# Placing an attention's transposes and value products later, and a few steps around them, in a one-core hybrid decoder layer

## The chip, the core and the metric

The kernel runs on one core of one Trainium2 chip. TensorE (PE) multiplies, VectorE (DVE), ScalarE (ACT) and GpSimd (POOL) do the elementwise work, and SyncE (SP) issues every transfer. The metric is the device time of one execution in microseconds, the median over several runs.

## The reference, cut to what matters

One layer of width 2048 over 512 tokens, all in float32. A normalized input is multiplied by one wide matrix, whose columns feed three kinds of branches (twelve heads of a delta-rule recurrence, twelve heads of an attention with a stick-breaking weight, and four pooling groups). The gated branch outputs go through one more matrix and are added to the input.

```
h = rms(x, norm_g)
proj = h @ w_in                      # 2048 columns in, 54 tiles of 128 columns out
pa, pb, pc = split(proj)
ya = rwkv7(token_shift(pa)) * silu(ga)          # per head: state recurrence over 512 steps
yb = pool(pu) * silu(pg)
# attention, per head:
q, k = rms(q, qn_g) * 64**-0.5, rms(k, kn_g)
z = q @ k.T                                      # strictly causal
after = reverse_cumsum(log_sigmoid(-z)) - log_sigmoid(-z)
w = exp(log_sigmoid(z) + after)
yc = (w @ v) * silu(gc)
x = x + concat(ya, yb, yc) @ w_out
```

## The kernel before

**The dense work.** The projection goes tile by tile: 128 columns of `w_in` against all 512 tokens. To reach float32 accuracy each operand is split into a high and a low part, and `three` (L454) issues three products for one: high by high, high by low, low by high. In the trace they are `pj<-hh,wh`, `pj<-hl,wh` and `pj<-hh,wl`. The first three tiles use weights that are split at the start. Each of the other 54 tiles takes two blocks of weights (128 x 1024 elements), so there are 108 blocks, each of 8 x 3 = 24 matmuls of 128 x 512; 32 blocks of `w_out` follow with the same count (`oacc`). Blocks are counted here from 0, the first one behind the three first tiles.

**A block's weights.** `split_weights` (L445) issues the load `raw` on SP's queue (two buffers), the cast `wh` on ACT (three buffers) and the remainder `wl = raw - wh` on DVE (two buffers). `weights(i)` (L477) asks for block i and block i+1, at a high scheduling priority (`AHEAD`). A buffer of `raw` is free again when the `wl` made from it is done, and a buffer of `wl` is free when the last matmul of its block has read it.

**The side work.** Everything else is written as Python generators: `begin`, six `rwkv(p)`, six `attention(p)`, four `pooling(g)`. After each dense matmul `pump` (L417) resumes those whose due time has come, and so their matmuls stand between dense matmuls in PE's order. The due time comes from a model of the engines (`Pace`): `need(tiles, tag, margin)` is the time at which the model has the named tiles ready and a bank of PSUM free, and then `margin` microseconds more (`MARGIN` is 2.5). A generator that yields `None` waits for a condition, for instance that the pair before has set a key in `done`. Four groups of banks are used: `pj` 2, `g` 3, `c` 2, `y` 1. The order on the other engines is a scheduler's, by the same program and its priorities; the engines then run their queues in that order.

**The steps around the change.**

- `emit_rstd` (L358) makes the reciprocal root of the row means: four scaled identities `dg` on DVE, a float32 product `rb` on PE, a copy `rstd` on DVE.
- `rwkv(p)`, L562 to L582: squares `sq` of the key, split into `sh` (ACT) and `sl` (DVE), and their sums over a head `ss` on PE. Further down are the products `gm`, DMAs of blocks out of `lt` to a scratch array `s1` and back as `nblk` and `xblk`, and a chain of 60 dependent small operations on DVE in which `pr` and `xblk` take turns (L681 to L687). They invert triangular blocks.
- `attention(p)`, L815 to L924: norm of query and key (`qs`, its split, `qm` on PE), then per head three groups of scores `z`, from each of which come `w`, `n`, `m` (ACT, POOL, two scans on DVE) and at the end the weights `w`. Behind the scores of both heads, in three groups of key blocks, the weights are transposed (`wT` on PE), copied to `wt` (ACT) and multiplied with the values (`o` on PE). The pair's end sets `done[("att", p)]`.

Of the kernel before, what the change touches and what calls it, by code (L numbers as in the profile page):

```python
# [8 lines left out]
F32 = mybir.dt.float32  # L9
# [4 lines left out]
P = 128  # L14
# [39 lines left out]
MARGIN = 2.5  # L54
TIGHT = 2.0
AHEAD = 300
# [161 lines left out]
def hybrid_trunk_kernel(ctx: ExitStack, tc: tile.TileContext, x, xT, w_in, w_out, vecs, consts, up_w, pool_w, out):  # L218
# [5 lines left out]
    def dma(out, in_, queue=nc.sync):  # L224
        pace.transfer(out, in_)
        queue.dma_start(out=out, in_=in_)
# [13 lines left out]
    def name(s):  # L240
        uid[0] += 1
        return f"{s}_{uid[0]}"
# [17 lines left out]
    def gb(s="g"):  # L260
        return bank("g", s)
# [96 lines left out]
    def emit_rstd():  # L358
        rt = cp.tile([P, 3, 4], F32, name="rt")
        ms, y0, t = rt[:, 0, :], rt[:, 1, :], rt[:, 2, :]  # L360
        dve.tensor_tensor(ms, xsum[:, 0, :], xsum[:, 1, :], ALU.add)
        dve.tensor_scalar(ms, ms, 1.0 / D, RMS_EPS, ALU.mult, ALU.add)
        act.activation(y0, ms, AF.Ln)
        act.activation(y0, y0, AF.Exp, scale=-0.5)
        dve.tensor_tensor(t, y0, y0, ALU.mult)
        dve.tensor_tensor(t, ms, t, ALU.mult)
        dve.tensor_scalar(t, t, -0.5, 1.5, ALU.mult, ALU.add)
        dve.tensor_tensor(y0, y0, t, ALU.mult)
        dg = tmp("dg")
        for i in range(4):  # L370
            dve.tensor_scalar(dg[:, i * P:(i + 1) * P], ident, y0[:, i:i + 1], None, ALU.mult)
        rb = gb("rb")
        pe.matmul(rb, ones_c, dg, start=True, stop=True)
        dve.tensor_copy(out=rstd, in_=rb)


# [65 lines left out]

    HK = KT // 2

    def split_weights(src):  # L445
        raw = wp.tile([P, HK * P], F32, tag="raw", bufs=2, name=name("raw"))
        dma(out=raw, in_=src)
        wh = wp.tile([P, HK * P], F32R, tag="wh", bufs=3, name=name("wh"))
        wl = wp.tile([P, HK * P], F32R, tag="wl", name=name("wl"))
        act.copy(out=wh, in_=raw)  # L450
        dve.tensor_tensor(wl, raw, wh.bitcast(F32), ALU.subtract)
        return wh, wl
# [19 lines left out]
    def fetch(i):  # L472
        if i < len(stream) and i not in fetched:
            with tc.high_priority(offset=AHEAD if i > 1 else 60):
                fetched[i] = split_weights(stream[i])

    def weights(i):  # L477
        fetch(i)
        fetch(i + 1)
        return fetched.pop(i)  # L480

    def project(n):
# [71 lines left out]
    def rwkv(p):  # L554
# [18 lines left out]
        mm(av, uph[:, P:2 * P], ad2, True, False)  # L573
        mm(av, upl[:, P:2 * P], ad2, False, True)
        a = sigmoid(av, bias=nvec[:, 6 + p:7 + p])
        yield need(*sqp, tag="g")
        ss = gb("ss")
        block_sum(ss, bone_r, sqp)
        rn = sq
# [233 lines left out]


    def attention(p):  # L815
        while p > 0 and not done.get(("att", p - 1)):
            yield None
        qk = []
        for kind, gain, slot in (("cq", nvec[:, 12:13], "aq"), ("ck", vec[:, V_KN:V_KN + 1], "ak")):
# [4 lines left out]
            sq = tmp("qs")  # L824
            act.activation(sq, raw, AF.Square)
            sqp = split(sq)
            yield need(*sqp, tag="g")
            ms = gb("qm")
            block_sum(ms, bmean_r, sqp)
            y0, t = newton_rsqrt(ms, RMS_EPS, eps_rms, sq)  # L830
# [6 lines left out]
        act.copy(out=kr, in_=k)  # L837
        klo = tmpr("klo")
        dve.tensor_tensor(klo, k, kr.bitcast(F32), ALU.subtract)
        head = []  # L840
        for h in range(2):
            s = slice(h * HD, (h + 1) * HD)
# [42 lines left out]
            if h == 0:  # L885
# [6 lines left out]
                for j in range(4):  # L892
                    transpose(vps[:, j * P:(j + 1) * P], vs[:, j * P:(j + 1) * P])
                act.copy(out=vt, in_=vps.rearrange("p (j c) -> p j c", j=4))

        o = None
        for js, width in (((0,), 512), ((1, 3), 512), ((2,), 256)):
            parts = []
            for h in range(2):
                yield need(*head[h].values(), tag="g", margin=MARGIN + 2.0)  # L900
                tps = gb("wT")
                pos = {}
                off = 0
# [6 lines left out]
                wt = ap.tile([P, T], F32, tag=home, name=name("wt"))[:, 0:width] if home else tmp("wt", width)  # L910
                act.copy(out=wt, in_=tps[:, 0:width])
                parts.append(wt)
            yield need(*parts, vt, tag="g" if o is None else None)
            if o is None:
                o = gb("o")
            for j in js:
# [106 lines left out]

    def begin():
        yield need(xsum, tag="g")
        emit_rstd()
        for n in range(NFIRST):
            finish(n, first[n])

# [134 lines left out]
```

## Time and profile before

| | before |
|---|---|
| median of 3 runs (lowest, highest) | 1008.57 us (1006.39, 1008.71) |
| the profiled execution, its span | 1007.96 us, 1006.1 us |
| PE busy | 978.3 us, 97% of the span |
| weight loads of PE (PEld, beside PE) | 786.9 us |
| DVE busy | 662.2 us, 66% |
| ACT busy | 511.6 us, 51% |
| POOL busy | 140.5 us, 14% |
| granted clock of PE | 0.996 |

The profiled execution is 0.6 us under the median. A matmul's end is modelled: a dense matmul is shown 0.39 us long though the next one starts 0.23 us after it, so the idle time shown in front of a late matmul is shorter than the time by which its start was late. A row of a timeline gives the start, the duration, the engine, the line, the operation with output and inputs, their shapes, the number of instructions, and in brackets the idle time in front of it and what ended that.

### The profile page before, as it was taken

To read this page: it belongs to the slowest core of one execution; us is meant where nothing else is said; L and a number is where in the kernel's file an instruction comes from. 1 tells how busy PE (TensorE), PEld (TensorE's weight loads), DVE (VectorE), ACT (ScalarE), POOL (GpSimd) and SP (SyncE) were. 2 spreads that over 40 slices of the span, in tenths; PEclk is the share of its full clock that TensorE was granted. 3 is DMA by queue.
4 is the path that set the end of the run, shared out by engine and by line. 5 is a ranking of instruction groups with operands and counts; after the bars stand their busy time and mean duration, and the time that the engine had idled before them with its cause. 6 is when DMAs were issued, how large, how long until landed. Compare 5 with 4: busy or idle time off the path is not lost. (4 is left out here: it accounts for less than half of the span.)

```text
span 1006.1 us, 13872 instructions
## 1 busy us (share of the span) xinstructions
PE 978.3 (97%) x5132; PEld 786.9 (78%) x5132; DVE 662.2 (66%) x1249; ACT 511.6 (51%) x838; POOL 140.5 (14%) x204
## 2 busy tenths in 40 slices
PE   8999999999899998999999999999999999999998
PEld 7867876888678886788768887788867888888886
DVE  5369784888849885697947979398864666323232
ACT  5656654756556654647546565466552245221210
POOL 0131211121120302112111111203211010000000
PEclk9999999999999999999999999999999999999999
DMA  9622322132321313223131222313232248624241
GB/s 337 216 90 76 103 85 90 63 111 68 105 84 58 114 65 106 79 84 95 64 121 64 90 89 80 105 63 110 72 106 79 98 145 281 219 87 147 93 138 63
DMA packets 62210, 109.17 MB, mean 109 GB/s; under 512 B 29760, under 2 KB 31168, under 8 KB 62144
## 3 DMA queue, kind: packets, MB, share of 16 engines
q1 hardware_dynamic: 62144, 108.30, 32.1%
q8 instruction: 40, 0.66, 0.3%
q14 instruction: 26, 0.21, 0.1%
HBM read 98.84 MB, written 9.44 MB: 108 GB/s over the span
## 5 line engine op out<-in xcount | busy, mean ns | idle before, releaser
L380 PE MATMUL pj<-hh,wl 128*128 128x512 f32 x864 | 343.7, 398 | 7.8 <-DVE wl L212 7.5
L380 PE MATMUL pj<-hh,wh 128*128 128x512 f32 x864 | 345.8, 400 | 0.1
L380 PE MATMUL pj<-hl,wh 128*128 128x512 f32 x864 | 343.4, 398 | 0.0
L212 DVE TENSOR_TENSOR wl<-raw,wh 128x1024 fp32r<-128x1024 f32 x140 | 174.4, 1246 | 174.6 <-PE oacc L380 86.1
L212 ACT CAST wh<-raw 128x1024 fp32r<-128x1024 f32 x140 | 146.4, 1046 | 205.7 <-PE oacc L380 95.2
L380 PEld LDWEIGHTS pj<-hh,wl 128*128 128x128 f32 x864 | 162.8, 188 | 45.7 <-DVE wl L212 12.4
L380 PEld LDWEIGHTS pj<-hh,wh 128*128 128x128 f32 x864 | 162.8, 188 | 33.6 <-issue 1.8
L380 PEld LDWEIGHTS pj<-hl,wh 128*128 128x128 f32 x864 | 163.0, 189 | 32.6 <-issue 2.2
L380 PE MATMUL oacc<-wl,yh 128*128 128x512 f32 x256 | 100.1, 391 | 0.0
L380 PE MATMUL oacc<-wh,yh 128*128 128x512 f32 x256 | 99.8, 390 | 0.0
L380 PE MATMUL oacc<-wh,yl 128*128 128x512 f32 x256 | 99.7, 390 | 0.0
L212 POOL TENSOR_SCALAR e<-e 128x512 f32<-128x512 f32 x28 | 45.2, 1614 | 197.4 <-ACT e L212 179.4
L380 PEld LDWEIGHTS oacc<-wh,yl 128*128 128x128 f32 x256 | 48.1, 188 | 10.3 <-issue 0.2
L380 PEld LDWEIGHTS oacc<-wl,yh 128*128 128x128 f32 x256 | 48.1, 188 | 10.2 <-issue 0.2
L380 PEld LDWEIGHTS oacc<-wh,yh 128*128 128x128 f32 x256 | 48.1, 188 | 10.0 <-DVE u L212 0.2
L212 POOL TENSOR_TENSOR d<-u 128x512 f32<-128x512 f32 x25 | 29.4, 1176 | 149.3 <-DVE xblk L212 67.6
L212 DVE TENSOR_TENSOR pr<-xblk,nblk 128x60 f32<-128x60 f32 (+8 forms) x180 | 46.5, 258 | 5.0
L212 ACT ACTIVATE e<-e 128x512 f32<-128x512 f32 x50 | 31.5, 630 | 35.7 <-POOL e L212 35.3
L212 DVE TENSOR_TENSOR_SCAN n<-n,m 128x512 f32<-128x512 f32 (+3 forms) x48 | 43.8, 923 | 7.5 <-ACT n L212 7.5
L212 DVE TENSOR_TENSOR xblk<-xblk,pr 128x60 f32<-128x60 f32 (+8 forms) x180 | 39.3, 218 | 5.0
L212 POOL CAST kl<-klo 64x512 fp32r<-64x512 f32 x24 | 19.2, 802 | 150.4 <-DVE klo L212 134.9
L212 ACT ACTIVATE n<-n 128x512 f32<-128x512 f32 (+1 forms) x72 | 39.6, 551 | 0.4
(203 smaller groups left out, 1227.5 us busy)
## 6 DMA issues: line engine op xcount, KB each, us to landing
raw<-in_w_in SPq DMA_DIRECT2D x108, 512.0 KB, 3.4
raw<-in_w_out SPq DMA_DIRECT2D x32, 512.0 KB, 3.4
lt<-in_x SPq DMA_DIRECT2D x8, 512.0 KB
xr<-in_x SPq DMA_DIRECT2D x16, 256.0 KB, 5.5
out<-xr SPq DMA_DIRECT2D x16, 256.0 KB, 4.1
yin<-yd SPq DMA_DIRECT2D x14, 256.0 KB, 4.6
fr<-in_w_in SPq DMA_DIRECT2D x12, 256.0 KB, 6.9
nblk<-s SPq DMA_DIRECT2D x24, 128.0 KB, 3.4
```

The lines of the kernel that those rows point to most:

```text
L212: return call(*args, **kw)
L380: pe.matmul(o, lhsT, rhs, start=start, stop=stop)
```

## The change

Eight edits, none of which adds or removes an instruction: each engine issues as many as before, in another order.

1. `rb` gets a due time of its own, `MARGIN + 2.0` behind `dg`, and goes through `mm`, so that the model counts its time.
2. The load `raw` is split off as `load_weights`, and `weights(i)` issues that of block i+2 as well, at the same high priority.
3. `ss` of the first pair gets 3.0 more margin.
4. The query and key norm of pair p starts when the scores of pair p-1 have been issued (`done[("scores", p-1)]`), not at that pair's end. The scores of pair p still wait for the end of pair p-1.
5. `qm` gets 1.5 more margin.
6. `wT` gets 2.0 more margin (`MARGIN + 4.0`).
7. `o` gets 1.5 more margin.
8. `emit_rstd` is a generator now, called by `yield from`.

```diff
         for i in range(4):
             dve.tensor_scalar(dg[:, i * P:(i + 1) * P], ident, y0[:, i:i + 1], None, ALU.mult)
+        yield need(dg, tag="g", margin=MARGIN + 2.0)
         rb = gb("rb")
-        pe.matmul(rb, ones_c, dg, start=True, stop=True)
+        mm(rb, ones_c, dg)
...
-    def split_weights(src):
-        raw = wp.tile([P, HK * P], F32, tag="raw", bufs=2, name=name("raw"))
-        dma(out=raw, in_=src)
+    raws = {}
+
+    def load_weights(i):
+        if i < len(stream) and i not in raws and i not in fetched:
+            raws[i] = wp.tile([P, HK * P], F32, tag="raw", bufs=2, name=name("raw"))
+            dma(out=raws[i], in_=stream[i])
+
+    def split_weights(i):
+        load_weights(i)
+        raw = raws.pop(i)
...
     def weights(i):
         fetch(i)
         fetch(i + 1)
+        with tc.high_priority(offset=AHEAD):
+            load_weights(i + 2)
         return fetched.pop(i)
...
-        yield need(*sqp, tag="g")
+        yield need(*sqp, tag="g", margin=MARGIN + (3.0 if p == 0 else 0.0))
         ss = gb("ss")
...
     def attention(p):
-        while p > 0 and not done.get(("att", p - 1)):
+        while p > 0 and not done.get(("scores", p - 1)):
             yield None
...
-            yield need(*sqp, tag="g")
+            yield need(*sqp, tag="g", margin=MARGIN + 1.5)
             ms = gb("qm")
...
         dve.tensor_tensor(klo, k, kr.bitcast(F32), ALU.subtract)
+        while p > 0 and not done.get(("att", p - 1)):
+            yield None
         head = []
...
+        done[("scores", p)] = True
...
-                yield need(*head[h].values(), tag="g", margin=MARGIN + 2.0)
+                yield need(*head[h].values(), tag="g", margin=MARGIN + 4.0)
                 tps = gb("wT")
...
-            yield need(*parts, vt, tag="g" if o is None else None)
+            yield need(*parts, vt, tag="g" if o is None else None, margin=MARGIN + 1.5)
...
-        emit_rstd()
+        yield from emit_rstd()
```

What this does to the order shows best in the third pair, where blocks 43 to 51 run. The numbers behind a name count tiles and operations; they differ between the two programs for the same thing.

On SP's queue, before, with `raw` of blocks 43 to 46 and the transfers of the recurrence between them:

```order
L226 DMA raw_529_3227<-in_w_in 128x1024
L226 DMA s1_510_3134<-lt0_98 32x8x32 x2
L226 DMA raw_546_3327<-in_w_in 128x1024
L226 DMA s1_510_3134<-lt0_98 32x8x32 x2
L226 DMA nblk_537_3263<-s1_510_3134 32x1024 x2
L226 DMA raw_561_3402<-in_w_in 128x1024
L226 DMA nblk_537_3263<-s1_510_3134 32x1024 x2
L226 DMA xblk_538_3264<-s1_510_3134 128x8x32
L226 DMA raw_568_3458<-in_w_in 128x1024
```

The same place on SP's queue now, with `raw` of blocks 43 to 46 again:

```order
L226 DMA raw_516_3159<-in_w_in 128x1024
L226 DMA s1_511_3125<-lt0_98 32x8x32 x4
L226 DMA raw_541_3272<-in_w_in 128x1024
L226 DMA nblk_532_3238<-s1_511_3125 32x1024 x4
L226 DMA xblk_533_3239<-s1_511_3125 128x8x32
L226 DMA raw_554_3361<-in_w_in 128x1024
L226 DMA raw_568_3434<-in_w_in 128x1024
```

The transfers of the recurrence stand ahead of the load of block 45 now; two of `nblk` and `xblk` stood behind it.

On DVE's queue, before, from `wl` of block 44 (`wl_548`) to the start of the inverse chain:

```order
L212 TENSOR_TENSOR wl_548_3330<-raw_546_3327,wh_547_3329 128x1024
L212 MEMSET xblk_538_3264 32x8
L212 TENSOR_TENSOR sl_544_3309<-yc_478_2948,sh_543_3308 128x512
L212 TENSOR_TENSOR pr_545_3313<-xblk_538_3264,nblk_537_3263 128x30
L212 TENSOR_TENSOR xblk_538_3264<-xblk_538_3264,pr_545_3313 128x30
L212 TENSOR_TENSOR pr_545_3313<-xblk_538_3264,nblk_537_3263 128x29
```

The same place on DVE's queue now, up to `wl` of block 44 (`wl_553`); ahead of these rows stand four more pairs of `pr` and `xblk`:

```order
L212 TENSOR_TENSOR pr_544_3295<-xblk_533_3239,nblk_532_3238 128x52
L212 TENSOR_TENSOR xblk_533_3239<-xblk_533_3239,pr_544_3295 128x2x26
L212 TENSOR_TENSOR pr_544_3295<-xblk_533_3239,nblk_532_3238 128x50
L212 TENSOR_TENSOR xblk_533_3239<-xblk_533_3239,pr_544_3295 128x2x25
L212 TENSOR_TENSOR sl_546_3318<-yc_479_2950,sh_545_3317 128x512
L212 TENSOR_TENSOR pr_544_3295<-xblk_533_3239,nblk_532_3238 128x48
L212 TENSOR_TENSOR xblk_533_3239<-xblk_533_3239,pr_544_3295 128x2x24
L212 TENSOR_TENSOR pr_544_3295<-xblk_533_3239,nblk_532_3238 128x46
L212 TENSOR_TENSOR wl_553_3358<-raw_541_3272,wh_552_3357 128x1024
```

The chain starts before `sl` and before `wl` of block 44 now, where it started behind both: eight of its `pr` stand ahead of that `wl`, none did. Behind `wl` of blocks 45, 46, 47 and 48 the count of `pr` issued was 9, 16, 26 and 28 of 30; it is 18, 23, 28 and 30 now.

On ACT's queue, before, around the copies `wt` of the second group (`wt_602`, `wt_607`) and the cast `wh` of block 51 (`wh_615`):

```order
L212 CAST wh_604_3699<-raw_603_3697 128x1024
L212 COPY wt_599_3669<-wT_598_3664 128x512
L212 ACTIVATE e_593_3643<-d_592_3640 128x512
L212 ACTIVATE e_593_3643<-e_593_3643 128x512 x2
L212 CAST wh_615_3762<-raw_614_3760 128x1024
L212 COPY wt_602_3695<-wT_601_3690 128x512
L212 COPY wt_607_3710<-wT_606_3705 128x512
```

The same place on ACT's queue now (`wt_603` and `wt_605` are the second group, `wh_620` is the cast of block 51):

```order
L212 COPY wt_593_3638<-wT_592_3633 128x512
L212 CAST wh_606_3715<-raw_600_3663 128x1024
L212 ACTIVATE e_596_3652<-d_595_3649 128x512
L212 ACTIVATE e_596_3652<-e_596_3652 128x512 x2
L212 COPY wt_603_3700<-wT_602_3695 128x512
L212 COPY wt_605_3711<-wT_604_3706 128x512
L212 CAST wh_620_3772<-raw_608_3719 128x1024
```

The two copies of the second group stand ahead of the cast of block 51 now; they stood behind it.

On PE, `rb` stands 7 dense matmuls later than before; in pairs two to five 56 to 61 matmuls stand between the pair's last scores (`z`) and the first group's transposes of the second head (`wT`), where 47 stood; between the second group's transposes and its `o` stand 23, where 16 stood.

## Rows read from the trace of the kernel before

**Rows 1.** The page, busy time: us, share of the span, number of instructions

```profile
PE 978.3 (97%) x5132; PEld 786.9 (78%) x5132; DVE 662.2 (66%) x1249; ACT 511.6 (51%) x838; POOL 140.5 (14%) x204
```

**Rows 2.** What PE waited for: us in total, times, longest

```profile
PE pj L380 <- DVE wl L212: 7.5, 8, 1.8
PE o L380 <- ACT wt L212: 4.4, 4, 1.7
PE wT L384 <- ACT w L212: 3.4, 4, 0.9
...
PE rb L373 <- DVE dg L212: 1.3, 1, 1.3
...
PE qm L380 <- DVE sl L212: 0.7, 1, 0.7
...
PE ss L380 <- ACT sh L212: 0.7, 1, 0.7
PE mu L380 <- DVE u L212: 0.4, 1, 0.4
```

**Rows 3.** Timeline of the third pair, around the first use of block 48's remainder

```profile
382.67 0.39 PE L380 MATMUL pj<-hl,wh 128*128 128x512 f32 x1
...
383.94 1.21 DVE L212 TENSOR_TENSOR wl<-raw,wh 128x1024 fp32r<-128x1024 f32 x1
384.03 0.39 PE L380 MATMUL pj<-hl,wh 128*128 128x512 f32 x1
...
385.21 0.50 PE L380 MATMUL pj<-hh,wl 128*128 128x512 f32 x1 [0.79 <-DVE wl L212]
385.23 0.33 SPq L226 DMA_DIRECT2D raw<-in_w_in  x1
```

**Rows 4.** Timeline of the third pair, ACT's queue ahead of the second value product

```profile
393.44 1.01 SPq L226 DMA_DIRECT2D raw<-in_w_in  x1
...
398.07 1.04 ACT L212 CAST wh<-raw 128x1024 fp32r<-128x1024 f32 x1 [2.00 <-DMA raw<-in_w_in]
399.02 1.06 ACT L212 COPY wt<-wT 128x512 f32<-128x512 f32 x2
399.65 0.54 PE L380 MATMUL o<-wt,vt 128*64 128x384 f32 x1 [1.42 <-ACT wt L212]
```

**Rows 5.** Timeline of the third pair, the transposes behind the last weights

```profile
387.87 0.55 PE L384 MATMUL wT<-kon,w 128*128 128x128 f32 x3 [0.89 <-ACT w L212]
```

**Rows 6.** Timeline, the first pair's key squares and their sum

```profile
67.00 1.05 ACT L212 CAST wh<-raw 128x1024 fp32r<-128x1024 f32 x1 [0.93 <-PE pj L380]
...
67.95 0.61 ACT L212 CAST sh<-sq 128x512 fp32r<-128x512 f32 x1
...
68.62 0.50 PE L380 MATMUL ss<-sh,bone_r 128*128 128x512 f32 x1 [0.73 <-ACT sh L212]
```

**Rows 7.** What SP's queue waited for: us in total, times, longest

```profile
SPq L226 <- DVE wl L212: 636.4, 123, 10.7
```

**Rows 8.** DVE in the dense stretch of the third pair: us, busy, granted clock, DMA share, GB/s

```profile
345.20:385.20 40.00, 35.94 (x88) 1.00 0.24 79
```

**Rows 9.** Timeline of DVE in the same stretch

```profile
353.45 1.22 DVE L212 TENSOR_TENSOR wl<-raw,wh 128x1024 fp32r<-128x1024 f32 x1
...
356.75 0.69 DVE L212 TENSOR_TENSOR sl<-yc,sh 128x512 fp32r<-128x512 f32 x1 [2.07 <-ACT sh L212]
357.36 0.18 DVE L212 TENSOR_TENSOR pr<-xblk,nblk 128x30 f32<-128x30 f32 x1
...
359.14 0.21 DVE L212 TENSOR_TENSOR pr<-xblk,nblk 128x52 f32<-128x52 f32 x1
```

**Rows 10.** Timeline of PE, late remainders in the first and the second pair

```profile
149.02 0.51 PE L380 MATMUL pj<-hh,wl 128*128 128x512 f32 x1 [1.35 <-DVE wl L212]
...
261.65 0.50 PE L380 MATMUL pj<-hh,wl 128*128 128x512 f32 x1 [1.20 <-DVE wl L212]
```

**Rows 11.** Timeline of PE, block 47's first use of its remainder

```profile
378.19 0.50 PE L380 MATMUL pj<-hh,wl 128*128 128x512 f32 x1
```

More of the change, by code (lines that the diff above doesn't have):

```diff
@@ L474, in fetch @@
             with tc.high_priority(offset=AHEAD if i > 1 else 60):
-                fetched[i] = split_weights(stream[i])
+                fetched[i] = split_weights(i)
     def weights(i):
```

## The prediction

> **What bounds the kernel now.** I read the page's busy times first, then what PE waited for, then the timeline around each kind of wait, and last the orders of the other engines there. The reader is to see in the first view that PE is the bound: 978.3 us busy, 97% of a span of 1006.1 us [rows 1]. No engine has more than 66% beside it, and since no instruction comes or goes, only PE's idle time can change. The second view says what that idle time is [rows 2]. Three causes make up most of it: DVE's remainders `wl` (7.5 us in 8 waits), ACT's copies `wt` in front of the value products (4.4 us in 4), ACT's weights `w` in front of the transposes (3.4 us in 4). Single waits follow.
>
> The time lost to a wait is a little longer than the idle time shown. In the third pair six steps from 382.67 to 384.03 make 0.227 us for a dense matmul; the late one starts 1.18 us after its predecessor, so 0.95 us were lost where 0.79 is shown [rows 3]. I add 0.16 us to every shown wait. So the three causes cost 8.8 us (7.5 + 8 x 0.16), 5.0 us and 4.0 us.
>
> **The change part by part.** The sum is made against the profiled execution, 1007.96 us; it lies 0.6 us under the median of the runs, and I add that at the end.
>
> *`rb`.* It waits 1.3 us for `dg` [rows 2], 1.4 us lost. It stands 7 dense matmuls later, 7 x 0.227 = 1.6 us: the wait goes, -1.4. What is late next would be the copy `rstd` and all that scales by it, but the generator's products stand later by the same amount.
>
> *Value products.* Distance from the second group's transposes to `o` grows from 16 to 23 matmuls, 1.6 us, more than three of the four waits. In the third pair the copies also stood behind the cast of block 51 on ACT: its load went out at 393.44, the cast ran at 398.07, the copies at 399.02, and `o` lost 1.42 us of shown idle time [rows 4]. In the new order the copies stand ahead of that cast. The longest wait, 1.7 us shown [rows 2], is 1.9 with the surcharge, so 0.3 of it is left: -4.7 of 5.0. The cast that now stands behind two copies starts 1.06 us later at most, and its block is used several microseconds later.
>
> *Transposes.* The four waits are alike, 0.9 us at most; in the third pair `wT` lost 0.89 us of shown idle time because `w` came late [rows 5]. With 9 to 14 more matmuls in front (56 to 61 for 47) PE arrives 2.0 to 3.2 us later, and 0.9 + 0.16 is less: -4.0.
>
> *Query and key norm.* `qm` waits 0.7 us once, for the first pair; it comes nearly a block later now: -0.9. Beside the earlier pair's end the next norm moves by about a block; its squares go into ACT's queue among the copies, each some 0.6 us. That is part of the allowance below. The wait of `mu` (0.4, with the surcharge 0.5) goes too, because its chain on DVE stands earlier: -0.5.
>
> *First key squares.* A larger margin should end the wait of `ss`, but it does the opposite in ACT's queue. Before, `sh` ran right behind the cast `wh` at 67.00 that had waited for a dense block's end, and `ss` waited 0.73 us for it [rows 6]. In the new order the square `sq`, which ran at 65.35 before that cast, stands behind it, and `sh` behind the square: some 1.2 us later against the block's end. PE's own order gives part of it back. I take +0.5, between 0 and +1.2.
>
> *Loads sooner.* By itself this is worth nothing. SP's queue spent 636 us in 123 waits for a `wl` [rows 7]: a load goes out when its buffer comes free, as at 385.23, right behind the `wl` that ended at 385.15 [rows 3]. Asking sooner cannot send it sooner. What it can do is block the queue for what stands behind; in the third pair the recurrence's transfers stand ahead of it instead.
>
> *Remainders.* The waits for `wl` come from DVE's order. In the third pair DVE is busy 35.94 of the 40.0 us from 345.2 to 385.2 [rows 8], and the remainder of block 48 starts at 383.94, one microsecond too late [rows 3]. The idle time in it has one large piece: 2.07 us at 356.75, when `sl` at the head of DVE's queue waited for ACT, and the inverse chain behind `sl` had not begun [rows 9]. In the new order twelve rows of the chain stand ahead of `sl`. A row takes 0.22 us (eight steps from 357.36 to 359.14), so 2.7 us of work fill those 2.07. Against it, by the order, priced row by row with its step in the trace, 0.7 us more work stand between the remainders of blocks 43 and 48, and 2.4 us more between 43 and 47. Block 48's remainder comes 2.07 - 0.7 = 1.4 us earlier and its wait of 0.95 goes; block 47's comes 0.3 us later and its wait grows by that: -0.7. The same reading for pairs four to six has the last remainder 4.7, 2.0 and over 5 us earlier: their waits go, 4.2 us with the surcharges. In the second pair it is half a microsecond, against 1.20 us shown at 261.65 and another behind it: -1.0 of 2.1. The first pair's 1.35 at 149.02 stays [rows 10]. Together -5.9 of 8.8; the ends of this term are -8.8 (all go) and +10 (the slower rival below).
>
> *New small waits.* Every product whose place moves can fall in front of its input. The rows show such single waits of 0.7, 0.7 and 0.4 us [rows 2]. Nothing in the trace of before says how many will be new; I allow one of 0.7 us in each of six pairs, +4.2, between 0 and +8.4.
>
> The sum: -1.4 - 4.7 - 4.0 - 0.9 - 0.5 + 0.5 - 5.9 + 4.2 = -12.7, hence 995.3 us for an execution like the profiled one, and 995.9 against the median. I say 996.
>
> **The rivals.**
>
> *The remainders stay late.* If the loads were already sent at once and DVE has the same work in the same dense stretch, the order may shift nothing. For it: 36 of 40 us busy, and waits that come back in each pair. The waits would then be a matter of capacity, two buffers of `wl` for instance. Against it: block 46's buffer is free before block 47's first use of its own remainder at 378.19 [rows 11], and block 48's remainder starts only at 383.94; it was DVE's queue and not the buffer. The time: 996 + 5.9 = 1002. The Trainium skill, "Perfetto Trace Analysis", section "Optimization Strategy", says that the same gap repeating on the engine that should be saturated can mean that too few buffers are there for the next tile. By that rule this rival would hold; the 5.7 us between those two rows speak against the rule here.
>
> *New waits eat the gain (no change).* The products of a pair share three banks, and `o`, later by up to a block, holds one longer while the next pair's norm asks for one. The trace of before shows no wait for a bank, so its cover is unknown. Two further waits of 0.9 us in each of six pairs, +10.4 with nothing else lost: 1006.
>
> *The chain runs over the remainders (slower).* On DVE the whole chain, all 30 `pr`, stands ahead of the remainder of block 48 now, where 28 stood; ahead of block 45's 18 stand where 9 did, some 4 us of work. This gets decisive if `xblk` lands or `sl` is ready later than the new order assumes, so that DVE stands still at the head of the chain and the remainders queue behind it. From 1.4 us of such idle time on the third pair loses; at 3 us in each of five pairs the term is +15 - 5 x 1.0 (the slack above, on average) = +10 in place of -5.9. 996 + 5.9 + 10 = 1012.
>
> **How the numbers follow.** Forecast, 989 to 1000: 0.55. Remainders stay, about 1002: 0.18. No change, 1003 to 1009: 0.15. Slower, 1010 and more: 0.12. A measurement of this kernel tells 0.3% (3 us) from no change, so faster begins under 1005.5: 0.55 + 0.18 + a third of 0.15 = 0.78. Within 0.3%: 0.10. Slower: 0.12. For 8 in 10 the range takes the forecast and the first rival, and part of the third case: 988 (every wait of the three kinds gone, no new one) to 1005. The forecast's own range is 989 to 1000.
>
> **What would show it.** In the list of PE's waits `wT` from `w` should be gone, `o` from `wt` under 0.5 us, `wl` near 3 us with one wait left in the first pair and one or two in the second; `rb` gone, `ss` about 1.2. DVE's idle piece in front of `sl` should be under 0.5 us. The forecast is wrong if `wl` keeps 7 us or more, or if new names with more than 5 us together appear in that list.

## The result and the profile after

| | before | changed |
|---|---|---|
| median of 5 runs each, in turn (lowest, highest) | 1008.71 us (1006.39, 1011.24) | 1014.69 us (1013.33, 1016.09) |
| ratio to before, 95% interval | | 1.0055 [1.0032, 1.0078] |
| profiled execution, its span | 1007.96, 1006.1 us | 1013.33, 1011.6 us |
| granted clock of PE | 0.996 | 0.993 |

The change makes the kernel 0.55% slower. The forecast, 996 us, was wrong in its sign, and 1014.69 lies above the range too. No engine got more instructions, and the first row of the page of the changed kernel (us, share, instructions) hardly differs from [rows 1].

```profile
PE 982.0 (97%) x5132; PEld 789.3 (78%) x5132; DVE 664.0 (66%) x1249; ACT 511.4 (51%) x838; POOL 143.9 (14%) x204
```

What PE waits for in the changed kernel (us in total, times, longest), against [rows 2]:

```profile
PE pj L381 <- DVE wl L212: 12.4, 9, 2.3
PE gm L381 <- DVE y L212: 2.1, 1, 2.1
...
PE ss L381 <- ACT sh L212: 1.9, 1, 1.9
PE s L381 <- DVE uv L212: 1.6, 4, 0.6
PE gh L381 <- DVE bx L212: 1.2, 1, 1.2
...
PE gm L381 <- DVE qs L212: 0.7, 1, 0.7
PE po L381 <- DVE pd L212: 0.7, 1, 0.7
```

`rb`, `qm`, `mu` and `o` from `wt` are gone from the list, and of `wT` one wait of 0.1 us is left: all that the moved products were to end has ended. In their place `wl` went from 7.5 to 12.4 us, and a row of new names stands there. With 0.16 us added to every wait, as in the prediction, and the clock's loss estimated from its mean over the span:

| step | predicted | measured |
|---|---|---|
| `rb` | -1.4 | -1.4 |
| value products `o` | -4.7 | -5.0 |
| transposes `wT` | -4.0 | -4.0 |
| `qm`, `mu` | -1.4 | -1.4 |
| first key squares `ss` | +0.5 | +1.2 |
| remainders `wl` | -5.9 | +5.0 (13.8 for 8.8) |
| new small waits | +4.2 | +8.3 |
| clock | 0 | +3.1 |
| sum | -12.7 | +5.8 |

The new small waits are 7.7 us shown in 12, 9.6 with the surcharge, less the 1.3 that `gm` and `s` cost before. The clock's term is (1 - 0.993) x 1011.6 = 7.1 us less (1 - 0.996) x 1006.1 = 4.0. The measured difference of the two profiled executions is 1013.33 - 1007.96 = 5.4 us; a wait of the first tiles, 2.6 us before and 2.0 now, is the rest but 0.2.

### The profile page after: what moved, and what is told of

Its sections match the earlier page's. It is cut to its first block, busy times and chain, and to the rows that moved or that the text cites. A ratio compares the mean times of both kernels' runs of the same rounds, so it can differ in the third digit from the quotient of the medians.

```text
span 1011.6 us, 13840 instructions
## 1 busy us (share of the span) xinstructions
PE 982.0 (97%) x5132; PEld 789.3 (78%) x5132; DVE 664.0 (66%) x1249; ACT 511.4 (51%) x838; POOL 143.9 (14%) x204
## 4 chain that ended last, share of the span: by engine, by line
PE 56%; DVE 25%; issue 9%; ACT 4%; POOL 3%; DMA 1%; SPq 0%; DVEq 0%; POOLq 0%; ACTq 0%
PE pj L381 27%; PE oacc L381 17%; DVE wl L212 5%; PE first L381 3%; DVE pr L212 3%; DVE xblk L212 3%; DVE bx L212 3%; POOL e L212 2%; DVE n L212 2%; ACT e L212 2%; DVE u L212 2%; PE o L381 1%; PE wT L385 1%; DVE bk L212 1%; DVE w L212 1%
## 5 line engine op out<-in xcount | busy, mean ns | idle before, releaser
L381 PE MATMUL pj<-hh,wl 128*128 128x512 f32 x864 | 346.2, 401 | 12.4 <-DVE wl L212 12.4
L212 POOL TENSOR_SCALAR e<-e 128x512 f32<-128x512 f32 x28 | 45.7, 1631 | 212.7 <-ACT e L212 206.8
L381 PEld LDWEIGHTS oacc<-wl,yh 128*128 128x128 f32 x256 | 48.0, 188 | 10.9 <-DVE wl L212 0.8
L381 PEld LDWEIGHTS oacc<-wh,yh 128*128 128x128 f32 x256 | 48.0, 188 | 10.8 <-ACT sq L212 0.6
L212 DVE TENSOR_TENSOR_SCAN n<-n,m 128x512 f32<-128x512 f32 (+3 forms) x48 | 40.6, 859 | 16.0 <-ACT n L212 14.8
L212 ACT ACTIVATE e<-e 128x512 f32<-128x512 f32 x50 | 31.4, 628 | 32.7 <-POOL e L212 32.4
L212 DVE TENSOR_TENSOR xblk<-xblk,pr 128x60 f32<-128x60 f32 (+8 forms) x180 | 41.8, 232 | 4.9
L212 ACT ACTIVATE w<-w 128x512 f32<-128x512 f32 (+1 forms) x36 | 20.1, 559 | 41.0 <-DVE w L212 39.3
```

The costliest lines, as they stand in the source:

```text
L212: return call(*args, **kw)
L381: pe.matmul(o, lhsT, rhs, start=start, stop=stop)
```

## The step that failed: the remainders

In the third pair the step seems to have come true. The timeline of the changed kernel there:

```profile
341.16 1.21 DVE L212 TENSOR_TENSOR wl<-raw,wh 128x1024 fp32r<-128x1024 f32 x1
...
344.49 0.58 DVE L212 TENSOR_SCALAR uv<-s,ec 64x64 f32<-64x64 f32 x2 [1.62 <-PE s L381]
346.37 1.32 DVE L212 TENSOR_TENSOR_SCAN n<-n,m 128x384 f32<-128x384 f32 x2 [1.30 <-ACT n L212]
...
349.24 1.23 DVE L212 TENSOR_TENSOR wl<-raw,wh 128x1024 fp32r<-128x1024 f32 x1
...
356.75 0.69 DVE L212 TENSOR_TENSOR sl<-yc,sh 128x512 fp32r<-128x512 f32 x1
...
379.64 1.22 DVE L212 TENSOR_TENSOR wl<-raw,wh 128x1024 fp32r<-128x1024 f32 x1
380.91 0.50 PE L381 MATMUL pj<-hh,wl 128*128 128x512 f32 x1 [1.02 <-DVE wl L212]
385.43 1.23 DVE L212 TENSOR_TENSOR wl<-raw,wh 128x1024 fp32r<-128x1024 f32 x1
```

The idle 2.07 us of `sl` [rows 9] are gone: no bracket stands at 356.75. From the remainder of block 43 (349.24) to that of block 48 (385.43) DVE now takes 36.2 us, where it took 38.6 (345.31 to 383.94), 2.4 less; I had said 1.4. (It is busy 0.9 us less between the two, where I had counted 0.7 us more, and idle 1.5 us less.) Block 48's wait [rows 3] is gone. But block 47 (379.64) is late by 1.02 us, because the stretch begins later. I had taken block 43's remainder for a fixed start. It is not: between it and the one before (341.16) DVE stands still for 1.62 us in front of `uv` and 1.30 us in front of the scan `n`, both at the head of its queue. Before, 2.35 us of idle time stood there too, but block 43's remainder was done 6.8 us ahead of its first use; now it is 4.3.

The other pairs went the same way. By the same reading I had the last remainder 4.7, 2.0 and over 5 us earlier in pairs four to six, and half a microsecond earlier in the second. From the remainders of blocks 59, 75, 91 and 27 to those of blocks 64, 80, 95 and 32, DVE takes 4.9, 2.3, 3.4 and 0.6 us less. So its pace was read about right, or too low as in the third pair, in every pair but the last, and it is the start that moved. Call lead the time by which a remainder is done ahead of its first use. Blocks 27, 43, 59, 75 and 91, with which the stretches began, had a lead of 5.9 to 6.8 us; it is 1.9 to 4.3 now. The first remainders to be late in pairs two to six are those of blocks 31, 47, 62, 79 and 94.

DVE in the fourth pair, changed kernel; the remainder at 468.00 is block 59's:

```profile
454.69 1.22 DVE L212 TENSOR_TENSOR_SCAN n<-n,m 128x512 f32<-128x512 f32 x1 [0.86 <-ACT n L212]
...
457.03 0.58 DVE L212 TENSOR_SCALAR uv<-s,ec 64x64 f32<-64x64 f32 x2 [0.29 <-PE s L381]
459.54 0.96 DVE L212 TENSOR_TENSOR_SCAN n<-n,m 128x384 f32<-128x384 f32 x1 [1.93 <-ACT n L212]
...
463.95 0.69 DVE L212 TENSOR_TENSOR sl<-yc,sh 128x512 fp32r<-128x512 f32 x1 [1.20 <-ACT sh L212]
464.56 0.18 DVE L212 TENSOR_TENSOR pr<-xblk,nblk 128x30 f32<-128x30 f32 x1
...
468.00 1.22 DVE L212 TENSOR_TENSOR wl<-raw,wh 128x1024 fp32r<-128x1024 f32 x1
```

The same place before; block 59's remainder is at 463.91:

```profile
463.17 0.58 DVE L212 TENSOR_SCALAR uv<-s,ec 64x64 f32<-64x64 f32 x2 [2.20 <-PE s L380]
463.91 1.23 DVE L212 TENSOR_TENSOR wl<-raw,wh 128x1024 fp32r<-128x1024 f32 x1 [0.15 <-ACT m L212]
...
475.34 0.69 DVE L212 TENSOR_TENSOR sl<-yc,sh 128x512 fp32r<-128x512 f32 x1 [2.07 <-ACT sh L212]
```

And PE from the first use of block 57's remainder to that of block 59's, first before, then in the changed kernel (window, us, busy, granted clock, DMA share, GB/s):

```profile
456.61:471.89 15.28, 15.28 (x85) 1.00 0.44 118
459.34:472.15 12.81, 12.81 (x63) 1.00 0.24 84
```

`sl` and twelve rows of the chain, which stood behind block 59's remainder, now run ahead of it: the stretch became shorter by work that moved ahead of its start. From block 57's remainder to block 59's DVE needs about as long as before, 16.6 us for 16.9. But PE needs 12.81 us for 15.28 from the first use of the one to the first use of the other, because 14 products of the side work stand between them in its order, where 34 stood. Block 57's own lead is smaller too, 6.7 us for 8.4. In pairs 2, 5 and 6 PE passes the same two blocks of its pair in 1.8, 2.4 and 2.4 us less, and DVE takes 0.9 to 1.0 us longer. In the third pair PE takes 0.4 us longer and DVE 0.6, and block 41's lead was already 2.2 us smaller.

Over the same blocks DVE stands still no longer than before, but for 0.9 us in the fifth pair. Its idle pieces above 0.1 us add up, before and now, to 5.5 and 5.3 us from block 26's remainder to block 31's, to 6.3 and 4.9 from 41 to 47, 6.3 and 4.6 from 57 to 63, 6.3 and 7.2 from 73 to 79, and 5.9 and 5.3 from 89 to 95. They stand elsewhere: `sl` still stands ahead of the chain in pairs 2, 4, 5 and 6 and waits 0.67, 1.20, 1.98 and 1.20 us, and the scans `n`, which had no wait in the fourth pair, wait 0.86 and 1.93 us for ACT's logarithms.

## The experiments

Ratios are to the kernel before, timed on the same chip beside it; the other numbers are those of the profiled execution. `wl` is the sum of PE's waits shown in the projection for remainders made on DVE (before 7.5, changed 12.4).

**Which edit.** The sooner loads taken out of the changed kernel (e1), done alone in the kernel before (e2), and the margins of `wT` and `o` taken back (e3):

```diff
 # e1; e2 is edit 2 of the change, alone
-        with tc.high_priority(offset=AHEAD):
-            load_weights(i + 2)
 # e3
-                yield need(*head[h].values(), tag="g", margin=MARGIN + 4.0)
+                yield need(*head[h].values(), tag="g", margin=MARGIN + 2.0)
-            yield need(*parts, vt, tag="g" if o is None else None, margin=MARGIN + 1.5)
+            yield need(*parts, vt, tag="g" if o is None else None)
```

> The changed kernel without the sooner load (edit 2); the other seven edits stay. Theory A (the loss comes from edit 2 alone, through the planner: told two blocks ahead when a block's weights land, it places the recurrence 1 to 2 blocks sooner, into the same blocks as the scores, and DVE reaches the remainders late): PE's waits for wl fall from 12.4 us to 8 or less, the waits of o and wT stay gone, time 1000 to 1006, at least 0.7% under the changed kernel. Theory B (the loss comes from the later transposes and value products and the earlier norm, edits 4 to 7): wl stays at 11 us or more, time 1010 or more.

> The kernel before with the sooner load (edit 2) and nothing else. Theory A: wl waits 11 us or more (8 before, 7.5 us), the waits of o and wT (4.4 and 3.4 us) stay as they were, so it is the slowest of all, 1013 to 1020. Theory B: wl near 7.5 us, time within 3 us of the kernel before.

> The changed kernel with the margins of wT and o as before (edits 6 and 7 undone). Theory A: wl waits stay near 12 us, o and wT wait 6 to 8 us again, time 1016 to 1022. Theory B: wl falls to 8 us, time 1007 to 1011.

Measured: e1 1010.08 us, 1.0006 [0.9993, 1.002], `wl` 12.0. e2 1019.02 us, 1.0103 [1.0088, 1.0118], `wl` 11.0. e3 1013.14 us, 1.0046 [1.0029, 1.0063], `wl` 11.0, `o` 1.7 and `wT` 1.5 back. What PE waits for in e1:

```profile
PE pj L381 <- DVE wl L212: 12.0, 9, 2.6
PE s L381 <- DVE uv L212: 2.4, 2, 1.3
...
PE gm L381 <- DVE bx L212: 2.2, 2, 1.5
PE ss L381 <- ACT sh L212: 1.9, 1, 1.9
```

and in e2:

```profile
PE pj L380 <- DVE wl L212: 11.0, 11, 2.7
PE gm L380 <- issue: 6.7, 1, 6.7
PE s L380 <- DVE bx L212: 3.7, 4, 0.9
```

The sooner loads cost 1.0% alone and about 0.5% in company, and are the one edit shown to be harmful. Most of the 1.0% is one wait, though: in e2 the first pair's `gm` stands a block earlier in PE's order (behind 6.0 blocks, 7.0 before, 6.8 in the changed kernel) and starts 6.7 us late, right behind `amr`, its last input. From DVE's timeline in e2:

```profile
88.14 0.69 DVE L212 TENSOR_TENSOR amr<-d,E 128x512 f32<-128x512 f32 x1
```

The expectation for e2 missed another thing: the waits of `o` are gone in it, and 1.2 of `wT`'s 3.4 us are left, without any later margin.

The other seven together are worth nothing (e1), though `o`, `wT`, `qm` and `mu` are gone there too: what they end comes back as `wl`, `s`, `gm` and `ss`. So the sooner loads alone don't make `wl` late; that part of the theory against them fell. But the late remainders of e1 are others: blocks 27, 43, 59, 75 and 91 keep a lead of 5.3 to 7.9 us in it, and nine blocks further on in the pairs are late (34, 48, 49, 65, 66, 80, 82, 97 and 98). Nor do the margins of `wT` and `o` gain what their waits had cost: without them the time is the same within the intervals.

How an edit can cost 10 us when its transfers don't start sooner: SP's queue in the changed kernel still waits 664.8 us for a `wl` (636.4 before [rows 7]), and 131 of 138 loads still leave within 0.1 us of their buffer's release (129 before). But the model that sets the due times (`Pace`) learns of a load two blocks ahead, expects the casts and remainders earlier, and places the side work by that. In PE's order the fourth pair's `gm` stands behind 56.1 blocks before, 54.5 in the changed kernel, 54.5 in e2, and 56.5 in e1. That is where the start of the stretch lost its lead: between the first uses of blocks 57 and 59 stand 34 side products before, 14 in the changed kernel and in e2, and 54 in e1, and block 59's lead is 6.8, 2.9, 2.9 and 7.9 us. A version that issues the load sooner but doesn't tell the model has, row for row on all engines, the order of e1; one that only tells it has the changed kernel's. These two were compared by their orders and not run.

**A third buffer of remainders** (e4), the rule that two are too few:

```diff
-        wl = wp.tile([P, HK * P], F32R, tag="wl", name=name("wl"))
+        wl = wp.tile([P, HK * P], F32R, tag="wl", bufs=3, name=name("wl"))
-TP = 16
+TP = 14
```

> The changed kernel with three buffers of wl for two, and 14 for 16 temporary tiles to make room; PE's order but for 6 rows is that of the changed kernel. If the remainders are late because DVE is busy or idle at the wrong moment (the order in its queue), a third buffer lets the remainder be made up to a block (5.5 us) sooner wherever DVE gets to it, and the waits of 0.4 to 2.3 us go nearly all: wl under 3 us, time 998 to 1004. If DVE simply has too much work in the dense stretch, a buffer changes nothing: wl 10 us or more, time 1012 to 1016.

Measured: 1019.48 us, 1.0105 [1.0088, 1.0122], granted clock 0.983. What PE waits for:

```profile
PE wT L385 <- ACT w L212: 5.6, 4, 2.2
PE q L381 <- ACT wt L212: 5.3, 1, 5.3
```

No `wl` is late any more, and the kernel is no faster than the changed one, where 998 to 1004 us were expected: the shown waits add up to 26.8 us (25.2 in the changed kernel), and they are longer, so the clock's term is (1 - 0.983) x 1018.3 = 17.3 us. As the first rival had it, the waits are "a matter of capacity" in that a buffer ends them; but what a late remainder held back then holds back others. With the third buffer two temporaries fewer were left (`TP`), so part of the new waits may be theirs.

**Two remainders per pair moved to POOL** in the changed kernel (e5), in the kernel before (e6) and in e1 (e8), to take 2.4 us per pair off DVE:

```diff
-        dve.tensor_tensor(wl, raw, wh.bitcast(F32), ALU.subtract)
+        if i % 16 in (11, 13):        # (12, 14) in e6 and e8
+            pace.record("dve", "tensor_tensor", wl, [raw, wh])
+            nc.gpsimd.tensor_tensor(wl, raw, wh.bitcast(F32), ALU.subtract)
+        else:
+            dve.tensor_tensor(wl, raw, wh.bitcast(F32), ALU.subtract)
```

> The changed kernel; two remainders wl of 16 (blocks 16k+11 and 16k+13, ahead of the late ones) are computed by GpSimd instead of VectorE, and the planner is still told VectorE: PE's order stays, but for 3 rows. Theory C (in the dense stretch of each pair VectorE's queue is the bound: its work plus its idle time waiting for ScalarE exceeds what PE gives it, so every microsecond of work or idle in it is a microsecond of PE): 2.4 us leave the queue per pair, wl waits fall from 12.4 to 3 to 5 us, time 1005 to 1008. Theory D (the remainder is late because of where it stands behind waiting rows, not because of the sum): wl falls by 3 us at most, time 1012 or more.

> The kernel before; two remainders of 16 (blocks 16k+12 and 16k+14) on GpSimd, planner told VectorE, PE's order unchanged. Theory C: wl waits fall from 7.5 us to 2 or less, time 1000 to 1004, better than both kernels. Theory D: wl falls by 2 us at most, time 1006 or more.

> The changed kernel without the sooner load, and two remainders of 16 (blocks 16k+12 and 16k+14) on GpSimd. Theory C: its wl waits fall from 12.0 us to 5 or less, time 1001 to 1005. Theory D: wl falls by 3 us at most, time 1007 or more.

Measured: 1.0293 [1.0256, 1.033] with `wl` 25.9; 1.016 [1.0132, 1.0189] with 20.9; 1.0173 [1.0151, 1.0195] with 17.2, beside 2.6 us for a remainder made on POOL. A miss: it doesn't relieve DVE. The timeline of DVE in e6:

```profile
376.36 1.10 DVE L212 TENSOR_TENSOR pr<-xblk,nblk 128x68 f32<-128x68 f32 x1
...
377.67 2.93 DVE L212 SCALAR_TENSOR_TENSOR d<-d,vec,u 128x512 f32<-128x512 f32 x1
...
380.52 0.21 DVE L212 TENSOR_TENSOR pr<-xblk,nblk 128x64 f32<-128x64 f32 x1
```

and that of POOL at the same time:

```profile
376.33 1.04 POOL L212 TENSOR_TENSOR d<-u 128x512 f32<-128x512 f32 x1 [10.52 <-DVE xblk L212]
...
377.63 2.42 POOL L453 TENSOR_TENSOR wl<-raw,wh 128x1024 fp32r<-128x1024 f32 x1
```

While POOL runs its 2.42 us, a `d` that takes 0.74 us elsewhere takes 2.93, and beside the 1.04 us of POOL's `d` a small `pr` takes 1.10 instead of 0.23. So these runs say nothing on DVE's capacity.

**Less work for DVE** (e11): the recurrence's bonus term is left out of the changed kernel, two DVE steps per pair, with the model told that they run:

```diff
-        dve.tensor_tensor(bv, bv, vs, ALU.mult)
+        pace.record("dve", "tensor_tensor", bv, [bv, vs])
-        dve.scalar_tensor_tensor(y, y, col(V_GNB), bv, ALU.add, ALU.add)
+        pace.record("dve", "scalar_tensor_tensor", y, [y, bv])
```

> The changed kernel without the two VectorE steps per pair that multiply and add the recurrence's bonus term (this part of the output is left out; the planner is still told of them): 0.66 + 0.74 = 1.4 us less work for VectorE in each dense stretch. Theory C: about 1.4 us less wl wait in each of five pairs, 12.4 to 6 us, and one half-clock stretch less: time 1004 to 1009. If the late remainders come from waiting for ScalarE and not from the sum of VectorE's work, the work removed becomes idle time: wl 11 us or more, time 1012 to 1015.

Measured: 1015.3 us, 1.0066 [1.0052, 1.0079], `wl` 10.9, DVE busy 656.4 (664.0). The run doesn't test what it was made for: DVE had as much to do between the remainders in question as in the changed kernel, 28.8 us for 28.3 from block 43's to block 47's, 21.0 for 21.0 from 59's to 62's, 27.4 for 27.4 from 75's to 79's and 21.5 for 21.4 from 91's to 94's. The two steps stand elsewhere, or, in the third pair, a scan that stood behind block 47's remainder took the place of one. On the sum of DVE's work the first two traces say more: over the same blocks it is larger in the changed kernel by 0.5 us in the third pair, by 0.1 in the second and in no other (28.5 for 28.4 us from block 27's remainder to block 31's, 28.3 for 27.8 from 43 to 47, 27.5 for 27.8 from 59 to 63, 27.4 for 27.8 from 75 to 79, 28.3 for 29.8 from 91 to 95).

**ACT's queue.** The four steps that make `n` and `m` put ahead in the changed kernel (e7); two of them, exponential and logarithm, left out (the attention's weights are then others) in the changed kernel (e17) and in the kernel before (e18):

```diff
+                with tc.high_priority(offset=SCAN):    # e7, around the four
                     act.activation(n, w, AF.Abs)
-                act.activation(n, n, AF.Exp, scale=-1.0)  # e17, e18
-                act.activation(n, n, AF.Ln, bias=1.0)
+                pace.record("act", "activation", n, [])
+                pace.record("act", "activation", n, [])
```

> The changed kernel with the four ScalarE steps that make n and m of a group of scores at a higher priority in ScalarE's queue (PE's order the same). Theory C with ScalarE as its cause: the idle time of VectorE in front of the scans n (2 to 4 us per pair) falls under 1 us, wl waits fall to 6 us or less, time 1006 to 1010. If the idle time only moves to another row, wl stays at 11 or more, time 1012 to 1017.

> The changed kernel without the exponential and the logarithm of n (two of four ScalarE steps per group of scores, 72 - 36 = 36 fewer; the attention's weights are other numbers; the planner is still told of them, PE's order is the same row for row). If the remainders are late because VectorE waits for n: its idle time in front of the scans falls from 2 to 4 us per pair to under 1, wl waits fall from 12.4 to 6 us or less, time 1004 to 1009. If the scans only show a lateness made elsewhere: wl 10 us or more, time 1012 to 1015.

> The kernel before with the same two steps left out. Its VectorE waits for n only 1.2 us in one pair. If n is the cause of what the change lost: wl stays at 5 to 7.5 us, time within 4 us of before, so that the two kernels without the steps differ by less than 2 us. If the steps are worth the same in both kernels, the difference between the kernels stays near 5.5 us.

Measured: e7 1016.0 us, 1.0065 [1.0043, 1.0086], `wl` 8.6, but a new `var` of 1.7 us, and the clock at 0.990. e17 1.0085 [1.0068, 1.0102], `wl` 11.5. e18 1.0042 [1.0027, 1.0057], `wl` 10.5 and `o` 9.4. In e17, with half of ACT's work for `n` gone, the scans still find DVE idle:

```profile
461.14 1.27 DVE L212 TENSOR_TENSOR_SCAN n<-n,m 128x384 f32<-128x384 f32 x2 [1.40 <-ACT m L212]
```

The order isn't the changed kernel's either: this row holds two scans, the second of which stood behind a remainder there. Behind the first 200 us, DVE's idle time in front of the scans adds up to 16.7 us in the changed kernel, 15.2 in e7 and 13.9 in e17, and to 1.2 in the kernel before and 13.1 in e18. So e7 and e17 didn't end the idle time they were aimed at, and e18 brought it into the kernel before, by another order of DVE's queue, with 3.0 us more of `wl`. e7 takes 3.8 us of `wl` away and gains nothing. These runs neither show ACT's work for `n` to be the cause nor rule it out.

**`sl`'s input sooner**: the copies `yc` and their split put ahead on ACT, in the kernel before (e9), in the changed one (e10), and in the kernel before with edit 7 (e12):

```diff
-                for h, s, o in quad:
-                    act.copy(out=yo[s], in_=y4[s, :, h, :])
+                with tc.high_priority(offset=AHEAD + 100):
+                    for h, s, o in quad:
+                        act.copy(out=yo[s], in_=y4[s, :, h, :])
-        yp2 = split(y)
+        with tc.high_priority(offset=AHEAD + 100):
+            yp2 = split(y)
```

> The kernel before; in ScalarE's queue only, the two copies of the recurrence's output yc and their split get a priority above the weight casts, so that the second copy of a pair runs ahead of the cast wh (blocks 45, 61, 77, 93) and not behind it. PE's order is the same row for row; 18 of VectorE's 1249 rows move. Theory C (VectorE is the bound of the dense stretch, its idle time in front of sl, 2.07 us per pair, is paid by PE): sl runs 1.05 us sooner, the idle piece falls to 1.0 us, and in each of four pairs the late remainder comes about 1 us sooner: wl waits 7.5 to about 4 us, time 3 to 5 us under the kernel before. Rival (the idle time would only appear in front of another row): wl stays at 7 us or more, time within 2 us of before.

> The changed kernel with the same priority for yc's copies and split; PE's order the same. VectorE waits for sl only 0.7 to 2.0 us there, and 2 to 4 us for n and uv, which this edit does not touch. Theory C: the idle time in front of sl falls in four pairs by up to 1 us each, wl waits 12.4 to 9 to 11 us, time 1010 to 1013. Rival: no change, 1014 to 1015.

> The kernel before with edit 7 alone (o's margin 1.5 us more, which leaves the pairs' places on PE as they were) and the priority for yc's copies. If both the wait of o (4.4 us) and part of wl's wait can go without moving a pair: o under 1.5 us, wl about 4 us, time 1000 to 1004, better than both kernels. If DVE takes the gain back, wl 8 us or more and time 1005 or more.

Measured: e9 1.0038 [1.0024, 1.0052], `wl` 8.2, `o` 6.8; e10 1.0043 [1.0023, 1.0063], `wl` 9.8; e12 1.002 [1.0008, 1.0031], `o` gone, `wl` 11.0, `s` 3.1. In e9 `sl` still waits 2.05 us: the cast of the next block came to stand between copies and split, so the edit missed its aim. e12 shows in small what the whole change does: the 4.4 us of `o` are gone, `wl` grows by 3.5 and `s` by 2.8.

**The first squares** (e15, changed kernel; e16, e1 with it): edit 3 undone.

```diff
-        yield need(*sqp, tag="g", margin=MARGIN + (3.0 if p == 0 else 0.0))
+        yield need(*sqp, tag="g")
```

> The changed kernel with edit 3 undone (margin of the first pair's ss as before). If the longer wait in front of ss and the half-clock stretch behind it come from that margin: ss 0.7 us for 1.9, that stretch gone, 2 to 3 us less, 1011.5 to 1013. If ss is late for another edit's sake: no change, 1014 to 1015.

> The changed kernel without the sooner load (edit 2) and without edit 3. By the same reasoning 2 to 3 us under the version without the sooner load (1010), that is 1006.5 to 1008.5, at or a little under the kernel before; or no change, 1009 to 1011.

Measured: 1.0074 [1.0057, 1.0091] with `ss` still 2.0, and 1.0019 [1.001, 1.0029] with `ss` 1.9. So edit 3 doesn't make `ss` late; that ACT's order is another does, through one of the other edits.

**What a wait costs** (e13, e14): the remainder of every third of the last blocks of `w_out` (118, 121, ... 139) computed six or seven times over, in the kernel before.

```diff
+        if i >= 118 and i % 3 == 1:
+            for _ in range(6 - 1):    # 7 - 1 in e14
+                nc.vector.tensor_tensor(wl, raw, wh.bitcast(F32), ALU.subtract)
```

> The kernel before; in the w_out stage, where PE waits for nothing and a remainder is 4.4 us early, the remainder of eight blocks (118, 121, ... 139) is computed six times over, which makes it about 1.4 us late. If a wait costs PE only its own length: +11 us in all (8 x 1.4). If a half-clock stretch follows each wait whatever its length: +20 us or more.

> The same with seven times over: about 2.6 us late, eight times. If a wait costs only its own length: +21 us. If waits beyond about 2 us are followed by a half-clock stretch of 1.2 to 1.6 us lost: +31 to +34 us, 10 to 13 us more than the idle times shown.

Measured: 1.0302 [1.0282, 1.0321] and 1.0473 [1.0455, 1.0491]. The row of these waits in e13 (us in total, times, longest):

```profile
PE oacc L380 <- DVE wl L454: 17.8, 8, 3.5
```

and in e14:

```profile
PE oacc L380 <- DVE wl L454: 28.4, 8, 5.3
```

The windows of PE in e13 around one of them, which starts 2.11 us late at 907.38 (window, us, busy, granted clock, DMA share, GB/s):

```profile
907.30:908.60 1.30, 1.22 (x4) 0.80 0.89 321
908.60:911.40 2.80, 2.80 (x8) 0.50 0.61 212
911.40:915.00 3.60, 3.60 (x17) 0.99 0.00 0
```

Behind the wait PE works at the lower of its two levels (1.2 GHz) for 2.8 us. Of the eight, the seven of 2.1 us and more have such a stretch behind them, the one of 1.1 us has none. The waits came out longer than aimed at, 2.2 and 3.6 us on average. In e13 they are 17.8 + 8 x 0.16 = 19.1 us and the clock's loss (1 - 0.988) x 1038.7 - 4.0 = 8.4, together 27.5 of 32.7 measured; in e14 29.7 + 16.0 = 45.7 of 48.4. By the clock's term a wait of this length cost 1.0 to 2.0 us beyond itself; 5.2 and 2.7 us of the measured times are left over.

## Why the prediction was wrong, point by point

*`rb`, `o`, `wT`, `qm`, `mu`* came out as worked out, -11.8 us for -11.5, for `o` and `wT` in part by luck. The reason given was the margins, and by the matmuls counted they are enough (e1). But in e2, which has none of them, `o` has no wait and `wT` 1.2 us, and in e3, the changed kernel without them, only 1.7 and 1.5 of the 4.4 and 3.4 us come back: most of these waits go in the new order without the margins. `rb` comes back by 0.2, 0.6 and 0.3 us in e7, e10 and e17, which have the changed kernel's order on PE but for two rows at most.

*`ss`* took the upper end, as read from ACT's queue: the square stands behind the cast. ACT's timeline in the changed kernel:

```profile
66.27 1.05 ACT L212 CAST wh<-raw 128x1024 fp32r<-128x1024 f32 x1 [2.06 <-PE av L381]
67.22 0.72 ACT L212 ACTIVATE sq<-d,vec 128x512 f32<-128x512 f32 x1
67.97 0.62 ACT L212 CAST sh<-sq 128x512 fp32r<-128x512 f32 x1
```

The prediction put it down to edit 3; e15 and e16 say that it isn't its doing.

*"By itself this is worth nothing"*, of the loads, was right on the transfers and wrong on the edit. The step left out who else reads the call: the model of the due times. e2 prices it at +1.0% alone, two thirds of that in one wait.

*Remainders* is the step that failed, by 10.9 us: -5.9 was predicted and +5.0 measured. It priced how long DVE takes from one remainder to the last late one, and took the lead of the first as fixed. The pace came out near the forecast or better but for the sixth pair (0.5, 1.4, 4.7, 2.0 and over 5 us earlier were read in pairs two to six, 0.6, 2.4, 4.9, 2.3 and 3.4 measured). What the runs showed in place of the fixed start: its lead fell from 5.9 to 6.8 us to 1.9 to 4.3, in pairs 2, 4, 5 and 6 mainly because PE comes to it 1.8 to 2.5 us sooner, with side products moved ahead. e1 and e2 tie this to the sooner loads. In none of these stretches had DVE stood still longer by more than 0.9 us. The slower rival, 1012 us, came nearest in time, and in part in kind: `sl` does hold DVE up ahead of the chain in four pairs. But its place was wrong: in three of the four `sl` waits ahead of the stretch and not in it, and the chain's head does not wait in the rows shown.

*New small waits* came out at the bound, 8.3 against 8.4. The second rival (whose 12 x 0.9 us make 10.8 and not 10.4) has its mechanism among them, once: a product of `gm` waits 2.1 us for the bank that `o` held and `y` reads last. From the changed kernel:

```profile
676.85 0.68 DVE L212 TENSOR_TENSOR y<-o,y 128x512 f32<-128x512 f32 x1
...
677.68 1.52 PE L381 MATMUL gm<-amr,bk 64*128 64x128 f32 x11 [2.08 <-DVE y L212]
```

*The clock* had no term, because I priced a wait at its length. Some waits cost more. PE's timeline in the changed kernel, around the late remainder of block 79:

```profile
616.53 0.78 PE L381 MATMUL pj<-hh,wl 128*128 128x512 f32 x1 [2.31 <-DVE wl L212]
617.11 0.63 PE L381 MATMUL pj<-hh,wh 128*128 128x512 f32 x1
617.54 0.63 PE L381 MATMUL pj<-hl,wh 128*128 128x512 f32 x1
```

and PE's windows there and behind another wait (window, us, busy, granted clock, DMA share, GB/s):

```profile
617.10:620.20 3.10, 3.10 (x9) 0.53 0.14 23
262.60:266.00 3.40, 3.34 (x15) 1.00 0.41 154
```

After 2.31 us of idle time the matmuls come every 0.43 us instead of 0.227 for 3.1 us. But behind a wait of 2.18 us at 262.66 the clock stays at 1.00, so a wait of 2 us can cost this and need not. The trace of before has two such stretches, behind waits of 2.60 and 1.77 us, and none behind one of 1.73; the changed kernel has four, behind 1.98, 1.93, 2.31 and 2.08 us, and none behind 2.18 and 2.20. Two more such stretches, each 3.4 us at a granted clock of 0.50, come to about the term of 3.1.

What stays open: what makes other remainders late in e1, where the starts keep their lead, so that the seven edits without the sooner loads gain nothing. The changed kernel and the fifteen of its or the kernel before's versions that kept two buffers and added no work (all but e4, e13 and e14) had 8.2 to 25.9 us of `wl` waits, against 7.5 in the kernel before (7.9 and 8.3 in e14 and e13, whose projection has its order), and none was faster than it; e1 ties. That the order before is simply a well-found one among many alike fits all of them, but it is argued and not shown.

## What to carry to other kernels

A margin that ends a wait re-plans every queue behind it: set against the waits it ends an allowance of about the same size for those that the new order brings (here 14.5 us came for 11.8 that ended). The time by which an engine is ahead depends on the one that waits for it as well: read both orders, in every repetition, from the last place where the late engine had time to spare. Ask of each edit who else reads what it touches, here a model that places work. And price a wait of 2 to 4 us on a saturated TensorE at about one and a half times its length (e13 and e14: 27.5 us for 19.1, 45.7 for 29.7), knowing that a single one may cost nothing more.

## What the runs showed of the hardware that was not expected

- An elementwise operation with two inputs on POOL can hold one on DVE up for its whole length: 2.93 us instead of 0.74 beside 2.42 us of POOL (e6). The Trainium skill, "SBUF — State Buffer", section "SBUF: two separate sides", says that the two engines lock a shared pair of ports against each other for a whole instruction when DVE has two inputs in SBUF and GpSimd reads it; the trace agrees.
- Seven waits of 2.1 us and more and one of 1.1 on a PE otherwise busy cost 8.4 us of clock beside their 19.1 us; eight longer ones 16.0 beside 29.7 (e13, e14).
